# MLP in eighths with seven block products for eight, and an in-place start, in a two-layer trunk kernel

## The chip, the cores and the metric

The kernel runs on 1 core of one Trainium2 chip. The time is the device time of that core in microseconds (us); every kernel is compared with the kernel before on the same chip. PE is TensorE, DVE is VectorE, ACT is ScalarE, POOL is GpSimd, SP is SyncE.

## The reference

Two layers over x of 512 frames by 1024 channels (float32). Each layer adds a mix of four head groups, a cross-attention over 256 memory rows, and an MLP of width 4096; a last RMSNorm follows.

```
for l in range(DEPTH):                                # DEPTH = 2
    h = rmsnorm(x, norm_mix[l])
    z = h @ w_in[l]                                   # split into the four groups
    ...                                               # retention, RG-LRU, latent attention, gated delta rule
    x = x + jnp.concatenate([y_a, y_b, y_c, y_d], axis=-1) @ w_out[l]
    x = x + memory_xattn(rmsnorm(x, norm_xattn[l]), rmsnorm(mem, norm_mem[l]), xa_wq[l], xa_wkv[l], xa_wo[l])
    h = rmsnorm(x, norm_mlp[l])
    x = x + jnp.square(jax.nn.relu(h @ mlp_w1[l])) @ mlp_w2[l]
return rmsnorm(x, final_norm)
```

## The kernel before

x lies transposed: eight tiles `xr[0]` to `xr[7]` of 128 channels by 512 frames. Every large product is made of three matmuls, since each fp32 operand is split into a high and a low part: `mm3_cm` (L288) issues high x high, high x low and low x high into one PSUM bank. Weights come from DRAM in units of 128 x 1024 words (512 KB), in the order of a list, `PLAN`. `wload` (L263) issues for a unit an SP DMA into `wr`, an ACT copy that rounds it to the high part `wh`, and a DVE subtract that gives the low part `wl`; `wnext` (L280) keeps this two units ahead. `wr` and `wl` have two buffers, `wh` has three.

The helpers record every operation, so that all matmuls have line L235 (`mm`), all DVE and POOL tensor_tensor L220 (`tt`), all activations L232 (`act`), scalar_tensor_tensor L223 (`stt`). Tiles are told apart by names. PSUM banks carry the tags `pj` (2), `gd` (2), `ch` (3) and `lg` (1). A scheduler orders the instructions of each engine by priorities of lanes.

**The start.** `norm_tile` (L373) makes from each `xr[k]` the parts `xh` and `xl`, and `square_acc` squares it on ACT (`sq`) and adds it into `acc`, on POOL for the first seven. The projection `gdn` reads four weight units (`proj_g`, L304); `rstd_of` (L384) sums `acc` over the partitions by matmuls, takes the inverse root by a bit trick and three Newton steps on DVE, and `bcast` (L394) spreads it by matmuls and an ACT copy (`bc`). The first step of the delta rule, `xt`, needs `bc`. `rope_tables` (L425), some 25 DVE operations of 128 x 128, is issued before layer 0.

**The MLP.** After `xo` (the output projection of the cross-attention) `norm_tile` makes `xh`, `xl` and `acc` for it. It runs in two halves of 2048 hidden channels. For each of 16 tiles of 128 channels, w1 takes 8 x 3 matmuls of 128 x 512 and an evacuation (ACT Relu `r`, DVE `s`, ACT `hh`, DVE `hl`); then w2 takes for each of 8 output tiles 16 x 3 matmuls of 128 x 512, DVE multiplies the bank with `r2` (the inverse mean square, from `rstd`) into `t_`, and POOL (first half) or DVE adds `t_` to `xr[m]`.

**The end.** `last_tile` does the eighth output tile of the last layer in two halves of 256 frames, sums squares into `acch`, takes the root, broadcasts it, multiplies all eight `xr` halves (DVE and POOL) and writes 16 DMAs from the SP queue.

Of the kernel before, what the change touches and what calls it, by code (L numbers as in the profile page):

```python
# [20 lines left out]
S = 512  # L21
NL = 2
# [25 lines left out]

class Spec:
# [6 lines left out]
KORD = (1, 3, 2, 0)  # L56
DIAG = ((0, 0), (1, 1), (0, 1), (1, 0))


def plan():  # L60
# [106 lines left out]
def build(tc, A, out, dbg=None):  # L167
# [92 lines left out]
    wstate = dict(loaded=0, used=0, tiles={})  # L260
    total = NL * len(PLAN)

    def wload():  # L263
# [72 lines left out]

    def rsqrt(o, v, n):
# [46 lines left out]
    def rstd_of(acc, ntt=TT):  # L384
        ps = sct()
        for t in range(ntt):
            mm(ps[:, t:t + 1], acc[:, t * 128:(t + 1) * 128], ones, True, True)
# [37 lines left out]
    def rope_tables():  # L425
        with tc.tile_pool(name="rp", bufs=1) as rp:
            N = TT * 32
            pf = rp.tile([128, TT], F32, name="pf")
            V.tensor_copy(pf, posi)
            h = rp.tile([128, N], F32, name="rh")  # L430
            lo = rp.tile([128, N], F32, name="rl")
            n = rp.tile([128, N], F32, name="rn_")
            tt(V, h.rearrange("p (t f) -> p t f", t=TT), pf.unsqueeze(2).to_broadcast([128, TT, 32]),
               C("invf").unsqueeze(1).to_broadcast([128, TT, 32]), MU)
            V.memset(lo, 0.0)
            big = 12582912.0
# [30 lines left out]
    def layer(l):  # L467
# [41 lines left out]
        with lane(*GDN):  # L509
            rstd = rstd_of(acc)  # L510
            rstdh = o16("rstdh", 4)
            ts(V, rstdh, rstd, 0.5, MU)
        pg = proj_g("gdn", xh, xl, [pjt, pjt, cht, cht])
        with lane(*GDN):
            rbc = bcast(rstd)
# [706 lines left out]
        def residual_proj(name, srch, srcl, gname, units=(0, 1, 2, 3), pre=None, post=None, new=None):  # L1222
# [13 lines left out]
        def last_tile(facc, hh, hl, r2):  # L1236
            ws = [wnext(f"w217_{k0}") for k0 in (0, 8)]
            pss = [pst(), pst()]
            accs, rs = {}, {}

            def prod(g, ks):
                s = slice(g * 256, g * 256 + 256)
                for k in ks:
                    wh, wl = ws[k // 8]
                    c = slice(k % 8 * 128, k % 8 * 128 + 128)
                    mm3_cm(pss[g][:, 0:256], wh[:, c], wl[:, c], hh[k][:, s], hl[k][:, s], k == 0, k == 15)

            def evac(g):
                s = slice(g * 256, g * 256 + 256)
# [251 lines left out]
```

## Time and profile before

| | us |
|---|---|
| median of 3 runs | 1639.4 (1637.24 to 1642.54) |
| time of the profiled execution | 1640.58 |
| its span in the trace | 1638.4 |
| PE busy | 1595.0 (97%) |
| DVE busy | 905.5 (55%) |
| ACT busy | 679.8 (41%) |
| POOL busy | 116.4 (7%) |

The span is the time between the first and the last record; 2.2 us of the profiled execution lie outside it. Busy times are sums over instructions. A chain row gives a start, a length and the instructions that ran one behind the other.

### The profile page before, as it was taken

How to read it: one execution, taken by the hardware profiler on the slowest of the kernel's cores; microseconds unless marked ns; L12 is line 12 of the kernel's file. 1: busy time of each engine (PE TensorE's matmuls, PEld its weight loads, DVE VectorE, ACT ScalarE, POOL GpSimd, SP SyncE). 2: the span in 40 equal slices, each digit the busy share in tenths (PEclk: the TensorE clock that was granted, in tenths of full speed). 3: DMA queues.
4: the chain of work that ended last, by engine and by line, in shares of the span. 5: the costliest groups of instructions: out<-in, count | busy, mean ns of one | idle time of the engine just before them, and what ended most of it. 6: DMA issues, size and time to landing. Idle time of an engine off the chain costs nothing.

```text
span 1638.4 us, 22678 instructions
## 1 busy us (share of the span) xinstructions
PE 1595.0 (97%) x8920; PEld 1330.1 (81%) x8920; DVE 905.5 (55%) x1949; ACT 679.8 (41%) x1163; POOL 116.4 (7%) x112
## 2 busy tenths in 40 slices
PE   6999999999999999999999999999999999999997
PEld 5868889888888888888887788988888888888886
DVE  6788688456455422443367957754564543234333
ACT  5556544344343312432335646444454432134331
POOL 2001000110110010000101000002002000100011
PEclk8999999999999999999999989999999999999998
DMA  4202034332122222233332111254312232333322
GB/s 162 94 26 66 24 104 139 132 116 78 52 94 100 90 98 96 91 102 109 124 99 68 52 53 59 82 168 129 102 40 90 91 103 90 97 96 96 98 91 77
DMA packets 47914, 150.61 MB, mean 92 GB/s; under 512 B 5696, under 2 KB 9792, under 8 KB 47808
## 3 DMA queue, kind: packets, MB, share of 16 engines
q1 hardware_dynamic: 47808, 149.16, 28.2%
q8 instruction: 70, 1.15, 0.3%
q14 instruction: 36, 0.29, 0.1%
HBM read 144.95 MB, written 4.19 MB: 91 GB/s over the span
## 4 chain that ended last, share of the span: by engine, by line
PE 85%; DVE 8%; DMA 3%; ACT 2%; issue 1%; POOL 0%; SPq 0%; POOLq 0%; ACTq 0%; DVEq 0%
PE ch L235 28%; PE pj L235 24%; PE gd L235 23%; PE lg L235 8%; DMA wr<-in_wu 2%; DVE wl L220 1%; PE ch L403 1%; DMA mem<-in_memT 1%; ACT wh L232 1%; DVE g L648 1%; DVE g L684 0%; DVE xt L223 0%; DVE xt L220 0%; DVE bf L229 0%; DVE g L220 0%
## 5 line engine op out<-in xcount | busy, mean ns | idle before, releaser
L220 DVE TENSOR_TENSOR wl<-wr,wh 128x1024 fp32r<-128x1024 f32 (+1 forms) x256 | 311.4, 1216 | 555.4 <-PE pj L235 174.1
L232 ACT ACTIVATE wh<-wr 128x1024 fp32r<-128x1024 f32 (+1 forms) x256 | 269.6, 1053 | 616.8 <-PE pj L235 190.8
L235 PE MATMUL pj<-xh,wh 128*128 128x512 f32 x288 | 115.2, 400 | 7.1 <-ACT wh L232 7.1
L220 POOL TENSOR_TENSOR acc<-acc,sq 128x512 f32<-128x512 f32 x42 | 64.9, 1546 | 765.5 <-ACT sq L232 765.5
L235 PE MATMUL pj<-xh,wl 128*128 128x512 f32 x288 | 114.8, 399 | 0.0
L235 PE MATMUL pj<-xl,wh 128*128 128x512 f32 x288 | 114.3, 397 | 0.0
L235 PE MATMUL ch<-xh,wh 128*128 128x512 f32 x272 | 106.9, 393 | 0.0
L235 PE MATMUL ch<-xl,wh 128*128 128x512 f32 x272 | 106.6, 392 | 0.0
L235 PE MATMUL ch<-xh,wl 128*128 128x512 f32 x272 | 106.4, 391 | 0.0
L235 PE MATMUL pj<-wl,xh 128*128 128x256 f32 (+1 forms) x352 | 105.9, 301 | 0.0
L235 PE MATMUL pj<-wh,xl 128*128 128x256 f32 (+1 forms) x352 | 104.7, 298 | 0.0
L235 PE MATMUL pj<-wh,xh 128*128 128x256 f32 (+1 forms) x352 | 104.3, 296 | 0.0
L235 PE MATMUL ch<-hh,wh 128*128 128x512 f32 x192 | 75.8, 395 | 0.0
L235 PE MATMUL ch<-hl,wh 128*128 128x512 f32 x192 | 75.8, 395 | 0.0
L235 PE MATMUL ch<-hh,wl 128*128 128x512 f32 x192 | 75.8, 395 | 0.0
L235 PEld LDWEIGHTS pj<-xh,wh 128*128 128x128 f32 x288 | 55.0, 191 | 18.6 <-ACT wh L232 7.1
L235 PEld LDWEIGHTS pj<-wl,xh 128*128 128x128 f32 x352 | 68.0, 193 | 2.2 <-issue 1.0
L235 PEld LDWEIGHTS pj<-wh,xl 128*128 128x128 f32 x352 | 68.1, 193 | 1.4 <-issue 0.7
L235 PEld LDWEIGHTS pj<-wh,xh 128*128 128x128 f32 x352 | 68.2, 194 | 1.1 <-issue 0.2
L220 DVE TENSOR_TENSOR hl<-s,hh 128x512 fp32r<-128x512 f32 x64 | 44.3, 692 | 39.2 <-ACT hh L232 39.0
L235 PEld LDWEIGHTS pj<-xh,wl 128*128 128x128 f32 x288 | 54.9, 191 | 12.1 <-DVE wl L220 0.8
L235 PEld LDWEIGHTS pj<-xl,wh 128*128 128x128 f32 x288 | 54.9, 191 | 11.1 <-DVE xl L223 0.2
(545 smaller groups left out, 3754.1 us busy)
## 6 DMA issues: line engine op xcount, KB each, us to landing
wr<-in_wu SPq DMA_DIRECT2D x248, 512.0 KB, 3.4
x<-in_xT SPq DMA_DIRECT2D x16, 256.0 KB, 3.6
wr<-in_wu SPq DMA_DIRECT2D x8, 360.0 KB, 2.9
mem<-in_memT SPq DMA_DIRECT2D x16, 128.0 KB, 3.2
xs<-x SPq DMA_DIRECT2D x8, 256.0 KB, 2.7
x<-xs SPq DMA_DIRECT2D x8, 256.0 KB, 3.0
out<-x SPq DMA_DIRECT2D x16, 128.0 KB, 1.8
big<-in_wmla SPq DMA_DIRECT2D x2, 640.0 KB, 6.4
```

The costliest lines, as they stand in the source:

```text
L220: e.tensor_tensor(o, a, b, op=op)
L232: ACT.activation(o, i, f, **k)
L235: PE.matmul(o, lhsT=l, rhs=r, start=st, stop=sp, **k)
L403: PE.transpose(o, i, ident)
L648: V.transpose(Nt3[32 * q:32 * q + 32].rearrange("m j i -> m i j"), src)
```

## The change

Four parts.

1. **Start.** DVE zeroes `acc`, and three matmuls of zeros run on PE ahead of the first product. The first weight unit is cut in two halves (DMA, ACT and DVE each). The squares are taken in place in `xr` (it is loaded again later, as before), and added on DVE, no longer on POOL. They are issued ahead of gdn's third unit, `rstd_of` ahead of the fourth, `bcast` behind it. The rope tables are issued behind `rstdh`, in a buffer of the delta rule. In layer 1 the root comes ahead of the third unit.
2. **w1 by seven products.** The operand x is cut into 2 x 2 blocks (channels 0 to 511 and 512 to 1023; frames 0 to 255 and 256 to 511), w1 likewise for each 256 hidden channels. `prep` forms four differences of x blocks for each pair of tiles (POOL for the first three pairs, DVE for the last), `combo` splits seven block operands into high and low parts. `wload` forms four sums of weight blocks (`sm`) on POOL, splits 768 raw columns into `ah`, `al` and the 1024 columns of sums into `wh`, `wl`. `sprod` issues for each unit 2 x 7 x 3 = 42 matmuls of 128 x 256, where before a unit took 24 of 128 x 512. `spost` puts the four result blocks together from four banks: an ACT copy `p1` and five DVE additions into `W`; `sact` does Relu, square and the split in one instruction each over 1024 columns.
3. **Eighths.** The MLP goes by 512 hidden channels: w1 of the next eighth interleaves with w2 of this one by units. After each eighth DVE multiplies 8 banks by `r2` into `t_` (2 buffers), and POOL adds `t_` to `xr` (DVE in the last eighth). `rstd_of` and `bcast` of the MLP come in eighth 1.
4. **End.** The last four tiles are done by (half, tile) blocks of 12 matmuls of 128 x 256; squares go into the sum by matmuls, not by additions; the root is ACT Sqrt, a reciprocal and one Newton step (`rsqrt1`); output DMAs alternate between the ACT and SP queues.

```diff
+def sw_units(name, w, c0, lead):
+    def unit(i, g):
+        ks, a, b = (2 * g, 2 * g + 1), c0 + i * 256, c0 + i * 256 + 128
+        blocks = [(k, a) for k in ks] + [(k + 4, a) for k in ks] + [(k + 4, b) for k in ks] + [(k, b) for k in ks]
...
+            raw = sw.tile([128, n], F32, tag="sr", name=nm("sr"), bufs=2)
...
+            tt(G, s1, a21, a22, AD)
+            tt(G, s2, s1, a11, SU)
+            tt(G, s4, a12, s2, SU)
+            tt(G, s3, a11, a21, SU)
...
+            act(ah, raw[:, 0:768], AF.Copy)
+            tt(V, al, raw[:, 0:768], ah.bitcast(F32), SU)
...
+            act(hi, sm, AF.Copy)
+            tt(V, lo, sm, hi.bitcast(F32), SU)
...
+    def rsqrt1(o, v, n):
...
+        act(o, v, AF.Sqrt)
+        ts(V, nv, v, -0.5, MU)
+        V.reciprocal(o, o)
+        tt(V, w, o, o, MU)
+        tt(V, w, w, nv, MU)
+        stt(o, w, 1.5, o, AD, MU)
...
+    for n in (512, 512, 256):
+        mm(wps[:, 0:n], warm[:, 0:128], warm[:, 0:n], True, True)
...
+    def first_acc():
+        for k in range(KT):
+            act(xr[k] if k else xg[2], xr[k], AF.Square)
+            if k:
+                tt(V, xg[2], xg[2], xr[k], AD)
...
+        def norm_in(u):
+            if l == 0 and u == 2:
...
+                    first_acc()
+            if u == (3 if l == 0 else 2):
...
+                    rs_["r"] = rstd_of(acc)
...
+        def sprod(h, i, g, bk):
+            ah, al, sh, sl = wnext(f"w1{h}{i}_{g}")
+            for dj in range(2):
+                j = 2 * g + dj
+                for n_, b_, x_ in PRD:
...
+                    mm(o, wh[:, c], cmb[j][0][x_], first, False)
+                    mm(o, wh[:, c], cmb[j][1][x_], False, False)
+                    mm(o, wl[:, c], cmb[j][0][x_], False, last)
+
+        def spost(bk):
...
+            act(p1, blk(bk[3], 0), AF.Copy)
...
+            tt(V, W7[:, 0:5:4, :], two(bk[0]), bc2(p1), AD)
+            tt(V, W7[:, 5:7, :], two(bk[1]), bc2(blk(W, 4)), AD)
+            tt(V, blk(W, 3), blk(bk[1], 0), blk(W, 6), AD)
+            tt(V, blk(W, 2), blk(bk[2], 0), blk(W, 6), AD)
+            tt(V, blk(W, 1), blk(bk[2], 1), blk(W, 5), AD)
...
+        def sact(C, hh, hl):
+            hi, lo = hp4(), hp4()
+            act(C, C, AF.Relu)
+            act(C, C, AF.Square)
+            act(hi, C, AF.Copy)
+            tt(V, lo, C, hi.bitcast(F32), SU)
...
+        setA = lambda: [bank(t) for t in ("pj", "pj", "gd", "gd")]
+        setB = lambda: [bank(t) for t in ("ch", "ch", "ch", "lg")]
...
+        def evac(m, ps, fin):
+            t_ = mp.tile([128, S], F32, tag="t_", name=nm("t_"), bufs=2)
+            tt(V, t_, ps, st["r2"], MU)
+            tt(V if fin else G, xr[m], xr[m], t_, AD)
...
+        for e in range(9):
...
+                    w1_unit(e, i, g)
+                    if e == 1 and q == 0:
+                        st["rstd"] = rstd_of(acc, new=lambda: bank("gd"))
+                if e:
+                    w2_unit(e - 1, q)
```

Where this puts instructions, at three places. In the changed kernel `tt` has line L234, `act` L246, `stt` L237, `mm` L249.

DVE at the start, before: behind the last `xl` the first rope operations (`rh`, `rn__186`, `rl`) stand ahead of the last addition into `acc`, the others between the steps of the root (`rv`, `rt` and what follows).

```order
L220 TENSOR_TENSOR rh<-pf,cst 128x128
L227 TENSOR_SCALAR spn_1760<-sp_365_1759 128x2
L229 TENSOR_SCALAR rn__186<-rh 128x128
L227 TENSOR_SCALAR sp_365_1759<-sp_365_1759 128x2
L227 TENSOR_SCALAR rn__186<-rn__186 128x128
L220 TENSOR_TENSOR acc_137<-acc_137,sq_173 128x512
L223 SCALAR_TENSOR_TENSOR rh<-rn__186,rh 128x128
L223 SCALAR_TENSOR_TENSOR rl<-rn__186,rl 128x128
L223 SCALAR_TENSOR_TENSOR rh<-rn__186,rh 128x128
L229 TENSOR_SCALAR rv_227<-gd_222 128x4
L229 TENSOR_SCALAR rn__186<-rh 128x128
L227 TENSOR_SCALAR rt_230<-rv_227 128x4
```

The same place now, from the last Newton step of the root on (`rw`, `rstd`): the rope operations (`rope_299`) begin behind `rstdh`, ahead of the first `xt`; the others follow between the next `xt` and `g` operations.

```order
L234 TENSOR_TENSOR rw_283<-rstd_281 128x4
L234 TENSOR_TENSOR rw_283<-rw_283,rn_284 128x4
L237 SCALAR_TENSOR_TENSOR rstd_281<-rw_283,rstd_281 128x4
L579 TENSOR_SCALAR rstdh_297<-rstd_281 128x4
L492 CAST rope_299<-posi 128x4
L495 MEMSET rope_299 128x128
L234 TENSOR_TENSOR rope_299<-rope_299,cst 128x128
L243 TENSOR_SCALAR rope_299<-rope_299 128x128
L241 TENSOR_SCALAR rope_299<-rope_299 128x128
L237 SCALAR_TENSOR_TENSOR rope_299<-rope_299 128x128 x3
L234 TENSOR_TENSOR xt_370<-pj_171,bc_364 128x512
```

What moved: the rope operations went from in front of and within the root to behind it; the seven additions into `acc` stand ahead of it, all on DVE.

DVE in eighth 2 (counted from 0), where w1 of a block of 256 channels ends and w2 of eighth 1 runs (`al`, and `wl` from `sm`: splits of the weight units to come; `W`: the result blocks; `t_`: output tiles). Behind each row stand the engines and queues that it waits for.

```order
L234 TENSOR_TENSOR al_5857<-sr_5849,ah_5856 128x768 [waits DMAHW2_49,PE_49]
L234 TENSOR_TENSOR W_5789<-pj_5637,p_1139_5790 128x2x256 [waits PE_49,Activation_49]
L234 TENSOR_TENSOR wl_5744<-sm_5734,wh_5743 128x1024 [waits DVE_49,PE_49]
L234 TENSOR_TENSOR W_5789<-pj_5638,W_5789 128x512 [waits DVE_49]
L234 TENSOR_TENSOR t__1145_5833<-ch_5704,r_1076_5415 128x512 [waits PE_49,Pool_49]
L234 TENSOR_TENSOR W_5789<-pj_5638,W_5789 128x256 [waits DVE_49]
L234 TENSOR_TENSOR W_5789<-gd_5639,W_5789 128x256 x2
L234 TENSOR_TENSOR t__1146_5836<-ch_5705,r_1076_5415 128x512 [waits PE_49,Pool_49]
L234 TENSOR_TENSOR t__1147_5839<-ch_5706,r_1076_5415 128x512 [waits PE_49,Pool_49]
L234 TENSOR_TENSOR wl_5799<-wr_5797,wh_5798 128x1024 [waits DMAHW3_49,PE_49,Activation_49]
L234 TENSOR_TENSOR t__1148_5842<-lg_5707,r_1076_5415 128x512 [waits Pool_49]
```

Every one of these is new in its place: a weight split (`wl_5744`) stands between the parts of `W`, and each `t_` from the second row on waits for POOL to have freed one of two buffers.

ACT in eighth 1, around the copy `bc` of the broadcast bank (`p_`: the copy `p1`; `W`<-`W`: Relu, then square; `hp`: high part).

```order
L246 ACTIVATE p_1068_5365<-gd_5186 128x256 [waits PE_49]
L246 ACTIVATE ah_5531<-sr_5524 128x768 [waits DMAHW4_49,PE_49]
L246 ACTIVATE wh_5373<-wr_5372 128x1024 [waits DMAHW3_49,DVE_49,PE_49]
L246 ACTIVATE W_5364<-W_5364 128x1024 [waits DVE_49]
L246 ACTIVATE W_5364<-W_5364 128x1024 [waits Activation_49]
L246 ACTIVATE wh_5444<-sm_5435 128x1024 [waits PE_49,Pool_49]
L246 ACTIVATE hp_5402<-W_5364 128x1024 [waits Activation_49]
L246 ACTIVATE bc_5413<-gd_5408 128x512 [waits PE_49]
```

Before, the same copy stood in half a, with 512-column evacuations around it; now it stands behind four 1024-column operations, and the bank that it reads (`gd`, of which there are two) is the one that the third product of the next w1 block takes.

## Rows read from the trace of the kernel before

**Rows 1.** The page: busy engines, granted clock in 40 slices, and the chain.

```profile
PE 1595.0 (97%) x8920; PEld 1330.1 (81%) x8920; DVE 905.5 (55%) x1949; ACT 679.8 (41%) x1163; POOL 116.4 (7%) x112
...
PEclk8999999999999999999999989999999999999998
...
PE 85%; DVE 8%; DMA 3%; ACT 2%; issue 1%; POOL 0%; SPq 0%; POOLq 0%; ACTq 0%; DVEq 0%
```

**Rows 2.** The chain in the MLP of layer 0: start us, length us, instructions.

```profile
500.67 5.44 PE ch L235 x24
...
566.26 11.20 PE ch L235 x48
```

**Rows 3.** The chain in the last product and its evacuation.

```profile
1612.38 5.70 PE pj L235 x48
```

**Rows 4.** Windows, layer 0's MLP: length, busy us of each engine, clock, DMA.

```profile
466.00:821.00 355.00, 355.00 (x1553) 290.01 (x1552) 147.76 (x178) 114.39 (x146) 20.48 (x20) 1.00 0.30 100
```

**Rows 5.** Groups by shape: busy us, mean ns of one, idle before.

```profile
L220 DVE TENSOR_TENSOR wl<-wr,wh 128x1024 fp32r<-128x1024 f32 x248 | 304.1, 1226 | 549.1 <-PE pj L235 171.3 <-PE ch L235 133.9 <-issue 93.9
L220 DVE TENSOR_TENSOR wl<-wr,wh 128x720 fp32r<-128x720 f32 x8 | 7.3, 907 | 6.3 <-PE pj L235 2.7 <-PE ch L235 2.1 <-ACT g L232 1.4
...
L220 DVE TENSOR_TENSOR t__1120_5579<-gd,r 128x512 f32<-128x512 f32 x1 | 0.7, 684 | 0.0
...
L220 DVE TENSOR_TENSOR o<-ch,bf 128x256 f32<-128x256 f32 x22 | 8.7, 417 | 0.3
...
L232 ACT ACTIVATE wh<-wr 128x1024 fp32r<-128x1024 f32 x248 | 263.2, 1061 | 609.9 <-PE pj L235 187.8 <-PE ch L235 184.5 <-PE gd L235 100.3
...
L220 POOL TENSOR_TENSOR xt<-xt,cst 128x256 f32<-128x256 f32 x6 | 4.0, 668 | 160.6 <-PE ch L403 79.5 <-DVE o L220 77.3 <-ACT mem L232 3.6
...
L220 POOL TENSOR_TENSOR x<-x,t__1120_5579 128x512 f32<-128x512 f32 x1 | 1.3, 1292 | 103.2 <-DVE t__1120_5579 L220 103.2
```

**Rows 6.** Timeline of DVE and POOL: start us, length us, idle before it.

```profile
12.65 1.81 POOL L220 TENSOR_TENSOR acc<-acc,sq 128x512 f32<-128x512 f32 x1 [2.58 <-ACT sq L232]
13.22 2.45 DVE L223 SCALAR_TENSOR_TENSOR xl<-x,par,xh 128x512 fp32r<-128x512 f32 x2
...
443.07 0.69 DVE L220 TENSOR_TENSOR x<-x,gd 128x512 f32<-128x512 f32 x1 [0.67 <-PE gd L235]
443.14 1.30 POOL L220 TENSOR_TENSOR acc<-acc,sq 128x512 f32<-128x512 f32 x1 [98.45 <-ACT sq L232]
```

**Rows 7.** Timeline of the start: PE, DVE, ACT.

```profile
7.07 0.80 PE L235 MATMUL pj<-xh,wh 128*128 128x512 f32 x1 [7.07 <-ACT wh L232]
...
12.74 0.40 PE L235 MATMUL ch<-xh,wh 128*128 128x512 f32 x1
...
26.37 0.28 DVE L223 SCALAR_TENSOR_TENSOR rh<-rn__186,rh 128x128 f32<-128x128 f32 x1
...
26.51 1.86 PE L235 MATMUL gd<-cst,acc 128*128 128x1 f32 x8 [6.79 <-DVE acc L220]
...
35.33 0.15 DVE L223 SCALAR_TENSOR_TENSOR rstd<-rw,rstd 128x4 f32<-128x4 f32 x1
...
37.43 0.60 ACT L232 ACTIVATE bc<-gd 128x512 f32<-128x512 f32 x1 [1.21 <-PE gd L235]
...
40.03 0.69 DVE L220 TENSOR_TENSOR xt<-pj,bc 128x512 f32<-128x512 f32 x1
```

**Rows 8.** The chain behind the start.

```profile
44.01 5.44 PE pj L235 x24
```

**Rows 9.** Timeline of the end.

```profile
1625.94 9.97 SPq L1267 DMA_DIRECT2D out<-x  x16
1626.28 0.61 PE L235 MATMUL gd<-cst,acch 128*128 128x1 f32 x4 [1.59 <-DVE acch L220]
...
1629.64 1.19 PE L235 MATMUL gd<-cst,rstd 128*128 128x128 f32 x4 [2.75 <-DVE rstd L223]
...
1631.34 1.75 DVE L220 TENSOR_TENSOR x<-x,gd 128x256 f32<-128x256 f32 x5 [1.85 <-ACT bc L232]
```

More of the change, by code (lines that the diff above doesn't have):

```diff
@@ L1220, in layer, with residual_proj @@
             SP.dma_start(out=xr[m], in_=A["xT"][:, m, :] if l == 0 else xs[m])
[L1222 removed]
+        def residual_proj(name, srch, srcl, gname, units=(0, 1, 2, 3), pre=None, post=None, new=None, order=range(8)):
             nonlocal xg
@@ new lines, in two_km @@
+        def two_km(e, half, k0):
+            wh, wl = wnext(f"w2{e}{half}k{k0}")
+            hh, hl = H[e]
+            if not k0:
+                st["W2"] = setB()
+            for m in range(4):
+                for dk in range(2):
+                    c = slice(dk * 512 + m * 128, dk * 512 + m * 128 + 128)
+                    mm3_cm(st["W2"][m], wh[:, c], wl[:, c], hh[k0 + dk], hl[k0 + dk], k0 + dk == 0, k0 + dk == 3)
+            if st["pend"]:
+                st["pend"].pop(0)()
+            return k0 > 0
@@ new lines, in w2_unit @@
+        def w2_unit(e, j):
+            half = "ab"[j // 2]
+            if e < 7 or half == "a":
+                if two_km(e, half, j % 2 * 2):
+                    if st["r2"] is None:
+                        b = bcast(st["rstd"], new=lambda: bank("gd"))
+                        st["r2"] = mp.tile([128, S], F32, name=nm("r2"))
+                        tt(V, st["r2"], b, b, MU)
+                    for m in range(4):
+                        evac(4 * (j // 2) + m, st["W2"][m], e == 7)
+                return
+            hh, hl = H[e]
+            if last:
+                if j == 2:
+                    last_tiles(st["facc"], hh, hl, st["r2"])
+                return
+            wh, wl = wnext(f"w2{e}{'bc'[j - 2]}k0")
+            for mi in range(2):
+                ps = cyb()
+                for k in range(4):
+                    c = slice(k * 256 + mi * 128, k * 256 + mi * 128 + 128)
+                    mm3_cm(ps, wh[:, c], wl[:, c], hh[k], hl[k], k == 0, k == 3)
+                evac(2 * j + mi, ps, True)
@@ new lines, in layer @@
+        for e in range(9):
+            if e == 8:
+                st["nx"] = nx = None if last else new_xg()
+                st["facc"] = xp.tile([128, S], F32, tag="acc", name=nm("acc")) if last else None
+            for q in range(4):
+                if e < 8:
+                    i, g = (q % 2, q // 2) if e == 0 else (q // 2, q % 2)
+                    if e == 0 and q == 3:
+                        for m in (2, 6, 3, 7):
+                            xo_sq(m)
+                    w1_unit(e, i, g)
[3 more added lines that the diff above has]
+                    w2_unit(e - 1, q)
```

374 lines of the change are left out of this document (235 added, 139 removed).

## Prediction

> **What bounds the kernel now.** The page comes first: PE is busy for 1595.0 of 1638.4 us, the clock row reads 9 almost throughout, and 85% of the chain that ended last is PE, against 8% DVE and 3% DMA [rows 1]. So the time is a number of matmuls times their spacing, plus the few places where PE waits. The chain by pieces gives the spacing. In w1 24 matmuls of 128 x 512 take 5.44 us, 226.7 ns each; in w2 48 take 11.20, 233.3 ns each [rows 2]. The only w2 tile that is done 256 frames at a time takes 5.70 us for 48, 118.75 ns each [rows 3]: half the columns cost 51 to 52% of the time. In the window over layer 0's MLP PE is busy for all of 355 us at full clock, with DVE at 147.76, ACT at 114.39 and POOL at 20.48 [rows 4]. Fewer columns on PE thus shorten the MLP, as long as the other engines keep pace. Outside it PE stands still at the start (6.79 us before the sums [rows 7]) and at the end.
>
> **w1.** A layer has 32 units. Before, 32 x 24 = 768 matmuls x 226.7 ns = 174.1 us. Now 32 x 42 = 1344 x 118.75 ns = 159.6 us: 14.5 less per layer, **-29.0** for two. That is not the full eighth (21.8 per layer), since short matmuls cost more per column. w2 keeps its 768 matmuls of 128 x 512, but in runs of 24 instead of 48; I leave it at 233.3 ns. If it ran like w1 it would give 768 x 6.6 ns = 5.1 per layer, 10.2 in all; that end is kept for the range.
>
> **The other engines in an eighth.** PE needs 4 x 42 x 118.75 ns + 4 x 24 x 233.3 ns = 42.4 us. Prices of [rows 5]:
> - DVE: four `al` of 768 columns (907 ns for 720, so 0.97) 3.9; four `wl` of sums and four of w2 at 1.226, 9.8; two `W` sets of 2 x 0.684 + 3 x 0.417, 5.2; two low parts of 1024 columns 2.5; eight `t_` at 0.684, 5.5. Sum 26.8.
> - POOL: 16 sums of 256 columns at 0.668, 10.7, and eight additions to `xr` at 1.292, 10.3. Sum 21.0.
> - ACT: four `ah` 3.2, eight `wh` 8.5, six 1024-column steps of the activation 6.4, two `p1` (an estimate: 0.38 for 256 columns, a quarter of `wh` and a little) 0.8. Sum 19.7.
>
> None reaches 42.4 alone. But DVE and POOL are not independent. At the start POOL adds from 12.65 to 14.46, and two `xl` of DVE that begin at 13.22 take 2.45 us, where DVE needs 0.684 for an operation of this size [rows 5]; at 443.07 a DVE addition that reads PSUM takes its 0.69 although POOL works from 443.14, and POOL its 1.30 [rows 6]. So an operation with both inputs in SBUF and a POOL operation exclude each other, one with a PSUM input does not. The Trainium skill, SBUF — State Buffer, section "SBUF: two separate sides", states this as a rule: a DVE operation with two SBUF inputs and a GpSimd operation that reads SBUF lock each other out for a whole instruction. By that rule the trace is explained (2.45 us against about 1.4 for two), and it speaks against a change that gives POOL more to do beside DVE. In a layer's MLP POOL goes from 20.48 us [rows 4] to 8 x 21.0 = 168. Here 16.1 of DVE's 26.8 us have two SBUF inputs (`al`, `wl`, low parts); with POOL's 21.0 the pair needs 37.1 of 42.4 us. It fits, with 5 us to spare.
>
> Fitting on average is not enough, since banks turn over. Let a w1 block end at T. DVE does `W` 0.68, a `wl` 1.23, `W` 0.68, a `t_` 0.68, then three `W` of 0.42 (the order fence of DVE), behind `p1` of 0.38 on ACT: the `gd` banks are free at about T + 4.9. PE has 24 matmuls of w2 (5.6) and two products (0.7) first, so it wants them at T + 6.3. The margin is 1.4 us, and one POOL addition in front of that `wl` or one late `t_` (two buffers, freed by POOL) takes 1.3 of it. Over some 30 such blocks I take **+4** in all; bounds are 0 and +20 (two POOL operations, 1.96, ahead at each block: 0.6 x 30 = 18).
>
> **Into w1.** Behind the last `xo` tile DVE has an addition, four differences and eight low splits for the last two pairs of tiles, some 8.4 us at [rows 5]; the units that need only the first two pairs, put first, keep PE for 2 x 4.99 = 10.0. Cost 0, bound +4 for both layers if POOL is late with its differences.
>
> **Root in eighth 1.** The w1 bank `gd` of the third product is the one in which `rstd` was spread. ACT frees it with `bc`, which stands behind `W` Relu, square, a `wh` and `hp`, all behind DVE's last `W` (the order fence of ACT). DVE's last `W`, with the small root operations between, is done at about T + 5.8; four ACT steps of 1.06 and `bc` (0.60 [rows 7]) follow, partly overlapping DVE: T + 10.4, where PE would want the bank at T + 7.2. Some 3 to 4 us per layer, with the one to two more us by which the weight split on DVE may be late: **+8** for two layers, bounds +2 (if ACT takes `bc` early) and +12. Nothing of it is in the trace of before, where the MLP ran through.
>
> **Start.** Before, the first product begins at 7.07, its first 12 matmuls last until 12.74, 0.47 us each, twice w1's 0.227, which is the lower of the clock's two levels (1.2 GHz) behind a PE that had done nothing; PE stands from 19.72 to 26.51 for DVE's last `acc`, the root ends at 35.33, `bc` begins at 37.43 and `xt` at 40.03 [rows 7], and PE leaves `gdn` at 44.01 [rows 8]. Now half a unit comes first, so the product can begin at about 6.1, behind the zeros, which I take to bring the full rate. Unit 1 waits for its split, which stands on ACT behind four conversions and two squares: 14.1. It ends at 19, unit 2 at 24.1; the squares and the seven DVE additions (0.68 each, as `t_`) are through at 24.4, the root, no longer interleaved with rope operations, at 28.9, unit 3 at 31.5. For PE that is 12.3 earlier. The delta rule's chain starts with `xt` at 30.8 instead of 40.03, 9.2 earlier, but some 25 rope operations (0.28, [rows 7], 7 us at most) are now between its first steps. What is passed on lies between: **-10.5**, bounds -6 (all rope operations on the chain, zeros of no use) and -13.
>
> **End.** From the sums to the last output: sums at 1626.28, then 2.75 us in which PE waits for the root, broadcast at 1629.64, products at 1631.34, end at 1638.4; the 16 output DMAs take SP's queue 9.97 us, 0.62 each [rows 9]. One Newton step instead of three and no bit trick makes 12 small operations 6, some 1.0; the last addition goes, 0.4; four of the last eight DMAs on a second queue are 1 to 2. **-3**, bounds -1 and -4.
>
> **Sum.** 1640.6 (the profiled execution; 1.2 above the median) - 29.0 + 4 + 8 - 10.5 - 3 = 1610.1. Taken against the median it would be 1609; I say **1610**.
>
> **Rivals.**
> - *No stalls* (chance 0.13): POOL fits into the gaps, `bc` is in time, and w2 in short runs goes like w1. 1640.6 - 29 - 13 - 4 + 2 = 1597, less up to 10: 1587 to 1600. For it: every average fits.
> - *The bank margin is too short* (0.22): `t_` with two buffers and POOL's additions hold `W` up in every block; +20 instead of +4 and +12 instead of +8: 1630, range 1617 to 1636. For it: 1.4 us of margin against 1.3 us operations. Against: most DVE work at that place reads PSUM.
> - *The start is not passed on* (0.08): the mix stage is paced by DVE, not by PE, and takes the rope operations in full: 1615 to 1621.
> - *DVE becomes the bound through POOL* (0.06): if DVE stood still for every POOL operation, an eighth would need 26.8 + 21.0 = 47.8 us, 5.4 over PE's, 86 over 16 eighths: 1692. It decides for slower from about 31 us over both layers, 1.9 per eighth, that is if POOL stops DVE for more than 17.5 of its 21.0 us per eighth. Range 1637 to 1692. The rule of the Trainium skill quoted above gives this case if it held for all of DVE's operations. Against: of DVE's work 10.7 us reads PSUM and isn't stopped.
>
> The forecast has 0.51 (its own range 1601 to 1617). The range for 8 in 10 goes from 1592, inside the first rival, to 1633, inside the second. Within 0.3% (5 us, about what a measurement can tell from no change) lies the edge between the second and the last rival: 0.03. Slower: 0.05. Faster: 0.92.
>
> **What would show it.** In the changed profile: w1 units of 42 matmuls in 4.99 us on the chain; PE busy near 97%; POOL's busy time up to some 440 us; DVE waits of `wl` and `al` behind POOL; one gap on PE of 3 to 4 us per layer released by ACT `bc`; the first `xt` near 31. Wrong it would be if the 256-column matmuls, four banks in turn, are further apart than 118.75 ns (3 ns are 8 us in all), if PE shows a gap at each block released by DVE `W`, or if the delta rule leaves its stage no earlier than before.

## The result and the profile after

The changed kernel takes 1620.6 us (median of 4 runs, 1619.25 to 1624.71) against 1640.0; the ratio is 0.9894, 95% interval 0.9875 to 0.9912. 1610 was forecast in a range of 1592 to 1633: the direction and the main term were right, and two thirds of the gain came. The page of the profile, as in [rows 1]:

```profile
PE 1574.2 (97%) x10094; PEld 1366.5 (84%) x10094; DVE 1134.7 (70%) x2197; ACT 784.2 (48%) x1269; POOL 502.2 (31%) x473
...
PE 74%; DVE 13%; issue 4%; ACT 3%; POOL 3%; DMA 3%; SPq 0%; POOLq 0%; DVEq 0%; ACTq 0%
```

PE lost only 21 us of busy time; POOL has four times its work, DVE a quarter more, and DVE, ACT and POOL have more of the chain (13, 3 and 3%; before 8, 2 and 0). Where the time came from is read by stages. In this table, worked out from the traces, a stage runs from the first matmul of one product to the first of the next: to `wout` of layer 0; `wout` and attention; `xo`; the MLP (its last matmul ends it); layer 1's mix stage, and in brackets the delta rule's solve inside it; and from the last product to the end of the span.

```
kernel                   mix 0  attn 0  xo 0  MLP 0   mix 1 (solve)  attn 1  xo 1  MLP 1   end     span
before                   287.2  135.2   43.5  355.2   267.6 (26.9)   135.9   43.5  355.9   14.2   1638.4
changed                  274.9  136.6   43.7  348.1   268.8 (25.5)   136.5   43.7  352.9   13.4   1618.5
e1 sums on DVE           275.2  135.3   43.7  347.1   265.9 (22.4)   135.2   43.7  351.9   12.8   1610.8
e2 differences on DVE    276.4  136.5   43.6  346.0   270.3 (26.8)   136.5   43.6  349.5   13.1   1615.6
e3 both on DVE           274.0  135.3   43.6  345.3   271.1 (28.4)   135.3   43.7  348.6   13.1   1609.8
e4 start alone           275.9  135.3   43.6  355.2   263.3 (22.4)   136.2   43.5  355.9   14.0   1622.9
e5 no zeros              278.0  136.6   43.7  348.4   268.1 (26.8)   136.5   43.7  354.8   13.3   1623.1
e6 sums twice            276.3  136.5   43.7  369.8   265.1 (22.4)   136.5   43.7  375.1   12.6   1659.3
e7 root a tile later     274.8  136.5   43.7  348.3   265.4 (22.5)   136.5   43.7  350.5   13.5   1613.0
e8 e3 and e7             275.7  135.2   43.7  344.4   270.0 (26.9)   135.3   43.7  345.7   12.9   1606.5
e9 e8, squares on DVE    275.5  135.2   43.6  340.5   263.6 (22.5)   135.2   43.6  342.3   13.9   1593.5
e10 long roots           273.5  136.5   43.7  348.2   271.2 (28.4)   136.5   43.7  353.3   15.2   1621.7
e11 e8, three buffers    273.4  135.2   43.6  343.1   265.3 (23.9)   135.2   43.7  345.4   13.2   1598.2
e12 e9 and e11           273.0  135.2   43.6  340.4   262.4 (22.5)   135.2   43.7  342.2   13.8   1589.6
```

The start gave 12.3, the MLPs 7.0 and 3.1, the end 0.8; attention took back 1.3 and 0.6, layer 1's mix stage 1.1. The solve's brackets move with the granted clock (last section) and belong to no kernel. Other stages also differ between profiles of the same instructions: mix 0 took 273.0 to 276.4 us in the twelve profiles with this start, so its 12.3 could be read as 10.8 to 14.3, and MLP 1 took 352.9 in the changed kernel and 354.8 in e5, which differs from it only at the start. Layer 0's MLP and attention repeat within 0.3 us.

**The steady MLP is as forecast.** Windows of the changed kernel: an eighth; all of layer 0's MLP, beside [rows 4]; and four stretches of the turn from `xo` to w1.

```profile
600.00:642.40 42.40, 42.40 (x266) 38.19 (x265) 29.54 (x32) 18.56 (x20) 25.61 (x25) 1.00 0.31 101
...
455.18:803.32 348.14, 343.14 (x2130) 308.05 (x2128) 247.67 (x288) 155.96 (x176) 200.06 (x183) 1.00 0.29 96
...
461.00:466.20 5.20, 5.17 (x43) 5.17 (x44) 2.68 (x3) 4.28 (x7) 5.08 (x6) 1.00 0.00 0
466.20:469.60 3.40, 0.31 (x3) 0.10 (x1) 3.40 (x7) 1.58 (x2) 0.69 (x1) 0.98 0.00 0
469.60:476.00 6.40, 6.37 (x41) 6.37 (x42) 4.95 (x5) 0.85 (x1) 2.71 (x4) 0.74 0.50 166
476.00:486.10 10.10, 10.10 (x85) 9.97 (x85) 8.04 (x14) 8.15 (x10) 8.99 (x9) 1.00 0.35 110
```

The columns are length, then busy us of PE, PE's weight loads, DVE, ACT and POOL, granted clock, DMA share and GB/s. An eighth of 42.4 us has PE busy for all of it: 118.75 and 233.3 ns per matmul hold. DVE and POOL stretch to 29.5 and 25.6 (26.8 and 21.0 were worked out): they stop each other, and it is hidden. The MLP of layer 0 is 1344 x 118.75 + 768 x 233.3 ns = 338.8 us of products and, as before, some 1.8 of root and broadcast; 7.5 us are lost, most of it in the turn (0.9 more is a wait of the first w2 product for its low part, at 486.5). There PE stands from 466.2 to 469.6, and then the mean clock is 0.74: 13 products are 0.213 us apart, the lower level (1.2 GHz), behind a PE that had stood 3.1 us.

**The turn.** Timeline of the changed kernel, from where DVE begins the splits for the third of the four pairs of tiles:

```profile
453.67 5.02 DVE L234 TENSOR_TENSOR cxl<-hp,cxh 128x512 fp32r<-128x512 f32 x4 [0.52 <-ACT cxh L246]
458.62 1.76 DVE L234 TENSOR_TENSOR wl<-sm,wh 128x1024 fp32r<-128x1024 f32 x1
460.30 0.67 DVE L234 TENSOR_TENSOR x<-x,lg 128x512 f32<-128x512 f32 x1
...
454.93 2.07 POOL L234 TENSOR_TENSOR hp<-hp,hp 128x256 f32<-128x256 f32 x2
456.96 2.33 POOL L234 TENSOR_TENSOR sm<-sr 128x256 f32<-128x256 f32 x2
459.26 1.71 POOL L234 TENSOR_TENSOR sm<-sm,sr 128x256 f32<-128x256 f32 x1
461.04 0.73 POOL L234 TENSOR_TENSOR sm<-sr,sm 128x256 f32<-128x256 f32 x1
...
461.81 1.06 ACT L246 ACTIVATE wh<-sm 128x1024 fp32r<-128x1024 f32 x1 [3.62 <-POOL sm L234]
462.78 0.71 ACT L246 ACTIVATE hp<-x,par 128x512 f32<-128x512 f32 x1
...
468.63 0.94 DVE L234 TENSOR_TENSOR al<-sr,ah 128x768 fp32r<-128x768 f32 x1
...
461.03 0.38 PE L249 MATMUL lg<-cxh,ah 128*128 128x256 f32 x1 [0.70 <-DVE x L234]
...
469.63 0.58 PE L249 MATMUL gd<-cxh,al 128*128 128x256 f32 x1 [3.12 <-DVE al L234]
```

Read it as two queues that hold each other up. Four splits, three of 0.69 and one of 0.42 us alone, take 5.02 us beside POOL's differences and sums, a `wl` 1.76 instead of 1.23, and POOL's third sum 1.71 instead of 0.67. So the last `xo` tile, done on PE by 455.2, is added to x on DVE only at 460.30. ACT meanwhile waits 3.62 us for POOL's last sum, with the scaling of that tile (`hp`, 462.78) queued behind the wait. The differences, splits and `al` of DVE come last, and PE waits for `al`.

**Attention.** The sums of the first two w1 units are prefetched into it:

```profile
394.72 1.44 POOL L234 TENSOR_TENSOR sm<-sr 128x256 f32<-128x256 f32 x2 [62.32 <-PE pj L249]
...
395.44 0.86 DVE L241 TENSOR_SCALAR Pm<-Pm,sm 128x256 f32<-128x256 f32 x1
396.23 0.69 DVE L234 TENSOR_TENSOR nb<-mx,nrs 128x1 f32<-128x1 f32 x1
```

In the kernel before the same two softmax steps took 0.35 and 0.15 us on average:

```profile
L227 DVE TENSOR_SCALAR Pm<-Pm,sm 128x256 f32<-128x256 f32 x32 | 11.0, 348 | 0.4
...
L220 DVE TENSOR_TENSOR nb<-mx,nrs 128x1 f32<-128x1 f32 x32 | 4.4, 150 | 0.1
```

The stage, which is a chain on DVE, gets 1.3 us longer in layer 0.

**The root in eighth 1** cost next to nothing: `bc` was late by 0.26 us, not 3 to 4.

```profile
508.10 0.38 PE L249 MATMUL gd<-cxh,ah 128*128 128x256 f32 x1 [0.26 <-ACT bc L246]
...
507.47 0.57 ACT L246 ACTIVATE bc<-gd 128x512 f32<-128x512 f32 x1
```

**The start**, beside [rows 7]: `xt` begins at 31.09, and PE begins the next unit at 32.50 instead of 44.01 [rows 8].

```profile
6.10 0.73 PE L249 MATMUL pj<-xh,wh 128*128 128x512 f32 x2 [0.34 <-ACT wh L246]
...
9.93 0.73 PE L249 MATMUL pj<-xh,wh 128*128 128x512 f32 x2 [2.17 <-ACT xh L246]
...
10.50 0.39 PE L249 MATMUL ch<-xh,wh 128*128 128x512 f32 x1
10.73 0.40 PE L249 MATMUL ch<-xl,wh 128*128 128x512 f32 x1
...
31.09 0.69 DVE L234 TENSOR_TENSOR xt<-pj,bc 128x512 f32<-128x512 f32 x1 [0.48 <-ACT bc L246]
```

**The end**, beside [rows 9]:

```profile
1597.09 0.35 PE L249 MATMUL gd<-cst,acc 128*128 128x1 f32 x2 [1.05 <-DVE acc L234]
...
1609.34 0.15 DVE L234 TENSOR_TENSOR rw<-rw,rn 128x2 f32<-128x2 f32 x1
1609.41 0.41 DVE L234 TENSOR_TENSOR x<-x,gd 128x256 f32<-128x256 f32 x1
1609.74 0.15 DVE L237 SCALAR_TENSOR_TENSOR rstd<-rw,rstd 128x2 f32<-128x2 f32 x1
1610.03 1.19 PE L249 MATMUL gd<-cst,rstd 128*128 128x128 f32 x4 [2.42 <-DVE rstd L237]
```

From 1595.75 to 1599.2 PE does one product; otherwise it waits for the sums of the first half's root and does their 12 one-column matmuls; 16 products behind it are 0.213 us apart. In the second half each small step of the root stands behind a 0.41 us product, so PE waits 2.42 us for a root of half the steps, 2.75 before.

### The profile page after: what moved, and what is told of

It is laid out like the page before. It is cut to its first block, busy times and chain, and to the rows that moved or that the text cites. A ratio compares the mean times of both kernels' runs of the same rounds, so it can differ in the third digit from the quotient of the medians.

```text
span 1618.5 us, 25948 instructions
## 1 busy us (share of the span) xinstructions
PE 1574.2 (97%) x10094; PEld 1366.5 (84%) x10094; DVE 1134.7 (70%) x2197; ACT 784.2 (48%) x1269; POOL 502.2 (31%) x473
## 3 DMA queue, kind: packets, MB, share of 16 engines
q10 hardware_dynamic: 1152, 1.05, 0.2%
## 4 chain that ended last, share of the span: by engine, by line
PE 74%; DVE 13%; issue 4%; ACT 3%; POOL 3%; DMA 3%; SPq 0%; POOLq 0%; DVEq 0%; ACTq 0%
PE ch L249 25%; PE pj L249 23%; PE gd L249 18%; PE lg L249 7%; DVE wl L234 2%; DMA wr<-in_wu 2%; POOL hp L234 1%; PE ch L454 1%; ACT wh L246 1%; POOL sm L234 1%; POOL acc L234 1%; DVE x L234 1%; DMA mem<-in_memT 1%; DVE Pm L241 0%; ACT hp L246 0%
## 5 line engine op out<-in xcount | busy, mean ns | idle before, releaser
L234 DVE TENSOR_TENSOR wl<-wr,wh 128x1024 fp32r<-128x1024 f32 (+2 forms) x193 | 257.5, 1334 | 228.8 <-issue 74.1
L246 ACT ACTIVATE wh<-wr 128x1024 fp32r<-128x1024 f32 (+2 forms) x193 | 201.4, 1044 | 252.9 <-DMA wr<-in_wu 74.8
L249 PE MATMUL ch<-hp,wh 128*128 128x512 f32 (+1 forms) x768 | 238.4, 392 | 0.9 <-DVE hp L234 0.9
L234 POOL TENSOR_TENSOR sm<-sr 128x256 f32<-128x256 f32 x128 | 99.7, 800 | 343.4 <-PE pj L249 133.4
L249 PEld LDWEIGHTS ch<-hp,wh 128*128 128x128 f32 x768 | 140.4, 189 | 29.3 <-DVE hp L234 1.5
L249 PE MATMUL ch<-hp,wl 128*128 128x512 f32 (+1 forms) x384 | 150.4, 392 | 0.0
L234 POOL TENSOR_TENSOR acc<-acc,sq 128x512 f32<-128x512 f32 x33 | 52.9, 1603 | 299.5 <-ACT sq L246 299.5
L246 ACT ACTIVATE wh<-sm 128x1024 fp32r<-128x1024 f32 x64 | 67.4, 1053 | 124.9 <-PE lg L249 110.7
L234 DVE TENSOR_TENSOR al<-sr,ah 128x768 fp32r<-128x768 f32 x64 | 89.4, 1397 | 50.4 <-PE gd L249 50.3
L246 ACT ACTIVATE W<-W 128x1024 f32<-128x1024 f32 x64 | 67.7, 1059 | 80.0 <-DVE W L234 79.1
L249 PE MATMUL pj<-wl,xh 128*128 128x256 f32 (+1 forms) x352 | 106.5, 303 | 0.0
L249 PE MATMUL pj<-wh,xl 128*128 128x256 f32 (+1 forms) x352 | 104.5, 297 | 0.0
L249 PE MATMUL pj<-wh,xh 128*128 128x256 f32 (+1 forms) x352 | 103.0, 293 | 1.4 <-DVE gd L237 1.3
L249 PE MATMUL pj<-cxh,wl 128*128 128x256 f32 x360 | 102.5, 285 | 0.4 <-DVE wl L234 0.4
L249 PE MATMUL pj<-cxh,wh 128*128 128x256 f32 x360 | 102.1, 284 | 0.0
L249 PE MATMUL pj<-cxl,wh 128*128 128x256 f32 x360 | 101.4, 282 | 0.0
L249 PEld LDWEIGHTS ch<-hp,wl 128*128 128x128 f32 x384 | 72.4, 189 | 16.1
L234 DVE TENSOR_TENSOR wl<-sm,wh 128x1024 fp32r<-128x1024 f32 x64 | 80.3, 1254 | 4.0 <-PE gd L249 2.9
L249 PE MATMUL lg<-hp,wh 128*128 128x512 f32 (+1 forms) x256 | 78.9, 390 | 0.0
L246 ACT ACTIVATE ah<-sr 128x768 fp32r<-128x768 f32 x64 | 53.9, 846 | 49.3 <-PE gd L249 37.2
L249 PE MATMUL gd<-cxh,al 128*128 128x256 f32 x240 | 68.4, 285 | 6.2 <-DVE al L234 6.2
L249 PEld LDWEIGHTS pj<-wh,xh 128*128 128x128 f32 x352 | 67.6, 192 | 2.9 <-DVE gd L237 1.8
```

What stands on the lines that cost most here:

```text
L234: e.tensor_tensor(o, a, b, op=op)
L246: ACT.activation(o, i, f, **k)
L249: PE.matmul(o, lhsT=l, rhs=r, start=st, stop=sp, **k)
```

## The experiments

Theory L: the missing 10 us are where POOL operations and DVE operations with two SBUF inputs shut each other out at places that nothing covers. Theory W: DVE and ACT simply have too much to do there. Ratios are to the kernel before on the same chip (its medians were 1638.7 to 1640.7 us), with 95% intervals. Only one execution of each kernel has a trace, so a difference by stages is one of that execution, not of the median.

**e1, the weight sums on DVE.**

```diff
-            tt(G, s1, a21, a22, AD)
+            tt(V, s1, a21, a22, AD)
```

(and so for `s2`, `s4`, `s3`).

> The four weight sums of each w1 unit go from POOL to DVE; the rest is the changed kernel (1620.6). Theory L (the changed kernel loses time where POOL operations shut DVE out: 1.3 us in each attention, 6 to 7 us in each turn from xo to w1): the attention loses its 1.3 us, the turn gets shorter by 1 to 3 us per layer, the steady eighths stay at 42.4 us (DVE has 33.5 of 42.4): 1612 to 1617. Theory W (the turn is long because DVE and ACT have too much to do there, whoever POOL is): eight more operations of 0.42 us stand on DVE in each turn, 3.4 us per layer: 1624 to 1629.

1609.4 us, ratio 0.9825 (0.9804 to 0.9846), below L's range. Attention is back at 135.3 and 135.2 us. In the changed kernel no engine waits there for a result of POOL's, so that loss was the exclusion itself. MLP 0 is 1.0 shorter, MLP 1 0.9, the low edge of L, and the eight more DVE operations per turn cost nothing net. But in the turn the wait moved. PE's wait before `al`, 3.1 us, is 0.1, and in layer 0 it now waits longer for `x` (0.70 before) and for `W` (none before):

```profile
461.52 0.39 PE L249 MATMUL lg<-cxh,ah 128*128 128x256 f32 x1 [2.16 <-DVE x L234]
...
479.94 0.39 PE L249 MATMUL gd<-cxh,ah 128*128 128x256 f32 x1 [1.99 <-DVE W L234]
```

So e1 bears out L in attention; in the turn it only shows that W's 3.4 us per layer did not come. Of the 7.7 us between the two traces 3.0 are the solve's.

**e2, the differences on DVE.**

```diff
-            E = V if j == 3 else G
+            E = V
```

> The differences of x blocks for the first three pairs of tiles go from POOL to DVE, as for the fourth; weight sums stay on POOL. Theory L: POOL's sums come some 5 us earlier in the turn, ACT's copy of them no longer holds up the last scaling of x, the idle 3.1 us of PE before al goes to below 1: 3 to 5 us less per layer, 1611 to 1615. Theory W: 4.6 us more on DVE per turn, PE idles longer: 1624 to 1630. The attention keeps its 1.3 us either way.

1616.9 us, 0.9864 (0.9844 to 0.9884), above L's range and far below W's. MLP 0 falls by 2.2, MLP 1 by 3.3, where L said 3 to 5. PE's wait of 3.1 us before `al` is 0.8 in both layers, as forecast, but waits of 0.9 and 0.8 us for W's banks stand in the trace; e5 and e7, whose MLPs up to the last tiles are the changed kernel's, have such waits too, so they are not clearly e2's doing. L's direction, at less than its size.

**e3, both.**

> Both moves: POOL is left with the squares of xo and the additions to x. Theory L: both gains, the PE gap at the turn below 1 us and the attention as before the change: 1606 to 1613. Theory W: 8 us more work on DVE per turn: 1630 or more.

1610.3 us, 0.9828 (0.9802 to 0.9854). W's 1630 is excluded. By stages it is better than e1 (MLPs 5.1 us less); in the traced executions its solve was 6.0 longer, so that the two spans are only 1.0 apart. What is left in the turn is a wait of PE of 2.1 us for `W`, in layer 0.

**e4, the start alone**, on the kernel before (the diff's parts on the first unit, zeros, squares, root and rope tables).

> The kernel before (1640.0) with the new start alone: halved first unit, zeros, squares in place on DVE, late broadcast, rope tables behind the root, and layer 1's root ahead of the third unit. If the start is passed on to the end in full, as the two traces' first product of wout says (287.23 before, 274.92 after: 12.3 earlier), 1627 to 1630. If the mix stage takes part of it back, 1631 to 1635. Layer 1's mix stage took 1.1 us longer in the changed kernel; if the earlier root there is the reason, it shows here too.

1624.6 us, 0.9911 (0.9892 to 0.9930), 14.4 less. Mix 0 gives 11.3; layer 1's mix is 4.3 shorter, of which the solve is 4.5. So the start is passed on in full, and the earlier root in layer 1 costs nothing there: the changed kernel's longer mix 1 is not its doing. By the medians the start alone has 14.4 of the changed kernel's 19.4 us. The other three parts, forecast at -20 together, are left with some 5, and the intervals of the two ratios overlap.

**e5, without the zeros.**

```diff
-    V.memset(warm, 0.0)
...
-    for n in (512, 512, 256):
-        mm(wps[:, 0:n], warm[:, 0:128], warm[:, 0:n], True, True)
```

> The changed kernel (1620.6) without the zeroing of acc and the three matmuls of zeros; the rest of the start is as changed. If the zeros bring the full rate to the first products, these run at half rate again: PE waits anyway until 9.93 for the second block of x, then some 12 to 25 products of unit 0 take 0.21 us more each, 2.5 to 5 us, and since PE went from unit 2 into the sums without a wait, most of it is passed on: 1622 to 1625. If the wait until 9.93 already undoes what the zeros did, or the sums have slack, within 1 us of the changed kernel.

1624.6 us, 0.9912 (0.9888 to 0.9935), as forecast, though this interval overlaps the changed kernel's. The trace is clearer: mix 0 is 278.0, 3.1 longer than in the changed kernel and 1.6 longer than in any of the twelve profiles with the zeros, and `xt` begins at 33.64, in those at 29.46 to 31.10. Its timeline of PE:

```profile
9.91 0.80 PE L249 MATMUL pj<-xh,wh 128*128 128x512 f32 x1 [2.14 <-ACT xh L246]
...
11.71 0.63 PE L249 MATMUL pj<-xh,wh 128*128 128x512 f32 x1
12.14 0.63 PE L249 MATMUL pj<-xl,wh 128*128 128x512 f32 x1
```

Products behind the same wait of 2.1 us start 0.43 us apart here and 0.23 in the changed kernel (10.50 and 10.73 above): zeros ahead of the wait buy the upper clock level (2.4 GHz) behind it. The level is read from the spacing, since the window views give a granted clock of 1.00 there in both kernels.

**e6, the sums twice** in eighths 2 to 7.

```diff
+            for _ in range(2 if int(PLAN[i][0][2]) > 1 else 1):
                 tt(G, s1, a21, a22, AD)
```

(with the other three inside the loop).

> In the w1 units of eighths 2 to 7 POOL makes the four weight sums twice (same values written again); nothing else. POOL goes to 31.7 us per eighth, beside PE's 42.4. Theory L with durations as they stand: DVE's operations with two SBUF inputs and POOL need 16.1 + 31.7 = 47.8 us, PE waits some 5 us in each of these eighths, 40 to 65 us in all: 1660 to 1685. Theory A (an average below PE's is hidden, exclusion or not): 1620 to 1625.

1662.2 us, 1.0141 (1.0114 to 1.0168): slower than the kernel before. PE's waits over the whole span, a window of 42.4 us, one of a whole eighth, and a wait of DVE:

```profile
PE ch L249 <- DVE wl L234: 19.0, 20, 1.0
PE pj L249 <- DVE wl L234: 14.9, 25, 1.7
...
600.00:642.40 42.40, 39.36 (x238) 34.30 (x237) 28.12 (x32) 14.79 (x17) 37.76 (x35) 1.00 0.25 87
587.90:634.30 46.40, 43.36 (x264) 38.04 (x264) 28.44 (x33) 18.56 (x20) 41.76 (x40) 1.00 0.27 91
...
601.95 0.69 DVE L234 TENSOR_TENSOR t__1215_6283<-ch,r 128x512 f32<-128x512 f32 x1 [5.63 <-POOL x L234]
```

DVE got no new work and is at 28 of 42.4, POOL at 38; neither is full, yet PE waits 34 us in all for DVE's `wl`. The eighth takes 46.4 us, and each MLP grows by 22 us, 3.6 per eighth on average. Theory A falls: an average below PE's is not hidden. The sum of what excludes itself, DVE's 16.1 and POOL's 31.7 us, is 47.8 and over PE's 42.4, where the changed kernel stood at 37.1. This is the last rival of the prediction, made real, with only part of DVE's work stopped. That the sum alone sets the 46.4 is not shown: DVE also stands 5.63 us at a `t_` until POOL's addition to x, queued behind the doubled sums, frees one of two buffers, and no run separates POOL's order from the sum.

**e7, the sums of the first half's root a tile later.**

```diff
-            rs[0] = rstd_of(p0, 2, rsqrt1)
             tile(1, 5)
+            rs[0] = rstd_of(p0, 2, rsqrt1)
```

> The changed kernel with the sums of the first half's root issued one tile of the second half later, at the end of the last layer. In the changed kernel's trace PE stands 1.1 us there for an addition on DVE, and the 16 matmuls behind run at half rate (0.213 us for 0.119). If the wait is the cause, the wait goes, and the time falls by 1 to 3 us: 1617.5 to 1619.5. If the one-column matmuls of the sums themselves are (12 of them, 2 us), nothing changes.

1614.7 us, 0.9855 (0.9830 to 0.9879), below the range expected. MLP 1 is 2.3 shorter, the wait of 1.05 us is gone (one of 0.47 for ACT's squares comes instead) and all but one of the products behind the sums are back at the upper level; 3.0 of the rest is the solve. The wait and the lower clock behind it were about half of the 4 us lost there.

**e8, e3 and e7 together.**

> Sums and differences on DVE and the root a tile later. If the gains add, 1 to 3 us under the run with both on DVE (1610.3): 1607 to 1609.

1608.2 us, 0.9804 (0.9774 to 0.9835). The gains add: MLP 1 345.7, solve 26.9.

**e9, the squares on DVE too.**

```diff
-        tt(G if k < KT - 1 else V, acc, acc, sq, AD)
+        tt(V, acc, acc, sq, AD)
```

> The kernel of the run with all on DVE and the root later (1608.2), with every addition of squares on DVE too, so that POOL is left with the additions to x in the MLP and the last products. Theory L: DVE's splits in the turn and in the last eighth are no longer stopped by 1.3 to 1.9 us additions: 1 to 4 us less, 1604 to 1607. Theory W: 14 more DVE operations of 0.68 in turn and end: 1609 to 1614.

1597.6 us, 0.9755 (0.9723 to 0.9786), below L's range. Of the 13.0 us between the traces of e8 and e9 the MLPs have 3.9 and 3.4, the solve 4.4, the rest of mix 1 2.0. Windows over both MLPs:

```profile
454.42:794.88 340.46, 340.46 (x2129) 306.54 (x2128) 284.48 (x407) 154.97 (x175) 82.15 (x62) 1.00 0.28 99
1237.32:1579.58 342.26, 342.26 (x2191) 310.43 (x2189) 284.66 (x417) 158.16 (x183) 80.00 (x56) 1.00 0.26 90
```

PE has no idle time in either: the 340.5 us are the 338.8 of products and 1.8 of root. DVE is busy 284 us, where it was 248 in the changed kernel. More DVE work and no wait: W is out. Only once, for 0.8 us, does ACT wait for a square of POOL's in the turn of e8, so here, as in attention, POOL beside DVE was most of the cost. For sums and differences the runs do not separate that from POOL being late with what ACT waits for (3.62 us in the changed kernel's turn): moving them takes both away.

Mix 1 without its solve is 241.1 us, 243.3 in the changed kernel. Its first root begins 16.6 us into the stage and its solve at 116.0 to 116.2 in all ten profiles with POOL's squares ahead of it; here, and in e12, they begin at 12.8 and 114.7. So 1.4 us go with the squares. The remainder lies behind the solve, where profiles differ from 125.3 to 127.4 us whatever POOL does (e5, with the changed kernel's instructions, has 125.3).

**e10, long last roots.**

```diff
-            rs[0] = rstd_of(p0, 2, rsqrt1)
+            rs[0] = rstd_of(p0, 2)
```

(and so for `rs[1]`).

> The changed kernel (1620.6) with the bit trick and three Newton steps in both last roots instead of Sqrt, reciprocal and one step. The prediction took 1.0 us for the short root. In the changed trace PE waits 2.42 us for the last root against 2.75 before, since each of its small operations on DVE stands behind a 0.41 us product of the first half: if these products set the pace, the long root costs 0.5 us or less more; if the number of operations does, 1 to 1.5 us more: 1621 to 1622.5.

1621.5 us, 0.9897 (0.9869 to 0.9924), no different by the median; by the trace the end is 15.2 instead of 13.4 (12.6 to 13.4 in the six profiles whose end is the changed kernel's), and PE's last wait for `rstd` 3.9 instead of 2.4. The number of steps does count: the short root is worth 1.5 us by the wait, 1.8 or more by the stage.

**e11, three raw buffers**, on e8.

```diff
-            raw = sw.tile([128, n], F32, tag="sr", name=nm("sr"), bufs=2)
+            raw = sw.tile([128, n], F32, tag="sr", name=nm("sr"), bufs=3)
```

> The kernel with all on DVE and the root later (1608.2) with three instead of two buffers for the raw w1 units. In its trace the fourth unit lands only after the second is given back, and its split falls together with the first W on DVE, for whose banks PE waits 1.7 us in layer 0. If the late landing is the cause, 0.5 to 2 us less per layer: 1604 to 1607. If DVE is simply full in the turn, no change.

1599.9 us, 0.9768 (0.9741 to 0.9794). In layer 0's turn PE's wait for `W` falls from 1.6 to 0.3 us, so the late landing was a cause; e9 loses the same wait without a third buffer. By the traces 8.3 us came: 1.3 in MLP 0, as expected, only 0.3 in MLP 1, and 3.0 in the solve, 2.3 in mix 0 and 1.7 in the rest of mix 1, which the edit does not touch.

**e12, e9 and e11 together.**

> The last two together: sums, differences and squares on DVE, the root a tile later, three raw buffers. With the squares on DVE alone layer 0's MLP takes 340.47 us where its matmuls need 338.8 and the root 1.8, so nothing is left there for a third buffer; layer 1's has 1.8 us more, some of it at the end. 1595 to 1599, not distinguishable from the run with squares on DVE (1597.6).

1594.4 us, 0.9755 (0.9730 to 0.9780), by the medians 44 us under the kernel before and 26 under the changed kernel, not told apart from e9.

## Why the prediction was right in direction and short in size

The number lies in the stated range, but above the forecast's own 1601 to 1617 and inside the ranges of two rivals, banks (1617 to 1636) and a start not passed on (1615 to 1621), neither of which happened. That it is not further off is partly luck: 12 us for banks and root, of which under 1 came, stood in for some 15 in the turns and 6 at the end that the sum did not have.

- **w1, -29.0, w2 unchanged.** Right to the row: 42.4 us per eighth, PE full. The products alone fall by 14.5 us per layer; in e9, where PE never waits, MLP 0 is 14.7 under the kernel before. (The prediction's sum for ACT, 19.7, adds up to 18.9; nothing rests on it.)
- **Banks, +4.** In the changed kernel's profile it was 0: the operations between the two `W` were stretched, but not beyond the margin of 1.4 us. The mechanism is real all the same, in the turn: e5 and e7 leave the MLP of layer 1 and of layer 0 as it is in the changed kernel, and PE waits there 1.25 and 0.89 us for a `W`. The waits of e6 are for `wl`, not for a bank.

```profile
1282.90 0.39 PE L249 MATMUL gd<-cxh,ah 128*128 128x256 f32 x1 [1.25 <-DVE W L234]
```

- **Into w1, 0.** This is the step that failed, in words "cost 0 ... the units that need only the first two pairs, put first, keep PE". It took most of 7.5 us per layer, where its bound was 4 for both. The 8.4 us of DVE work were priced as if alone; with the weight splits and waits between them they take from 453.67 to 470.18, twice that, while POOL makes differences, sums and squares, and ACT's wait for a sum was not seen at all. The prediction had stated the exclusion and applied it only to the average of an eighth. e9 shows the loss vanish with POOL's work moved away, at more DVE work.
- **Root in eighth 1, +8.** It was 0.5 in all. The wait is the one forecast, the term was too large: PE's wish for the bank was put at T + 7.2, and it came at T + 8.8 (508.1 less the wait of 0.26, in a block that ended at 499.1), since the broadcast's own matmuls and more products run ahead of it; ACT had `bc` done at T + 9.0.
- **Start, -10.5.** 12.3 to `wout`, inside the bounds; PE left `gdn` 11.5 us earlier, not 12.3, and `xt` came 8.9 earlier, not 9.2. The delta rule's solve began only 6.1 earlier (129.46 for 135.53), so between `xt` and the solve some of the lead is spent, whether on rope operations was not taken apart; by `wout` it is back. e4 bears out that the start is passed on, e5 what the zeros do.
- **End, -3.** From the last product on it was -0.8, and the wait for the first half's root with the slow products behind it took about 4 before that: +3 net. The root's shortening was sized at 1.0 and is worth at least 1.5 (e10), so other parts of the new end cost about 1 more than the old; which of them (12 one-column matmuls for 4, products between the root's steps) was not taken apart.
- **Not in the sum:** 1.3 and 0.6 us in attention, from POOL beside a chain of DVE (e1), and about 2.5 in layer 1's mix stage without its solve, of which 1.4 go with the squares on POOL (e9) and the rest differs between profiles.

The Trainium skill, SBUF — State Buffer, section "SBUF: two separate sides", states the exclusion for single instructions, and so it has to be asked at each place where a DVE chain is on the path, not of the mean. The trace agrees, with 0.69 for 0.15 us on a 128x1 operation. The Trainium skill, Perfetto Trace Analysis, section "Optimizing Scalar/DVE Operations", warns that moving work between DVE and GpSimd may not help; here moving it back to DVE, with the later root, gave 23 us by the medians (1620.6 to 1597.6) and 25.0 by the traces, 18.3 of them in the MLPs and 3.0 in the solve.

## What to carry to other kernels

Add up what excludes itself: DVE operations with two SBUF inputs and POOL's operations share one budget. Beside 42 us of PE a sum of 37 cost nothing in the steady eighths here, and one of 48 cost 3.6 per eighth; where between them the loss begins no run shows. Where DVE's chain is the path itself (a softmax, a turn between stages, a root), POOL beside it costs at once, and there an operation is better on DVE for 0.42 us than on POOL for 0.67. Price a turn between two stages as its own stage, with each queue's order written down. And before a difference of stages is given a cause, see how far that stage moves between profiles of the same instructions.

## What the runs showed of the hardware

The solve of the delta rule in layer 1 issues the same instructions in the same order on PE, DVE, ACT and POOL in all fourteen profiles, and takes 22.4 to 28.4 us. The windows around it, of e1 and of e3:

```profile
915.40:940.84 25.44, 23.67 (x380) 22.28 (x378) 19.42 (x35) 14.14 (x25) 2.25 (x4) 1.00 0.25 84
```

```profile
912.12:943.49 31.37, 29.60 (x380) 27.96 (x379) 19.43 (x35) 14.14 (x25) 2.24 (x4) 0.78 0.19 68
```

DVE and ACT have the same busy time, PE 5.9 us more, and the granted clock is 1.00 against 0.78: for part of the stretch PE runs at the lower of its two levels (1.2 GHz). Over the fourteen profiles the length follows the granted clock within the solve: 22.4 to 22.5 us at 1.00, 23.9 at 0.93, 25.5 at 0.87, 26.8 to 26.9 at 0.81 and 28.4 at 0.76, with PE idle for 1.7 to 1.8 us in each. What PE did ahead of it is the same in e1 and e3: it stands 1.0 us for ACT ahead of the solve and 1.7 for DVE inside it, and then does 62 small matmuls of 64 x 64. The products behind these are 0.12 us apart in e1 and 0.21 in e3. In layer 0 the same solve took 24.4 to 24.7 us at granted clocks of 0.93 to 1.00, with less idle time on PE at the lower one (0.2 us instead of 1.3). So a difference of 3 us between two medians, or 6 between two profiles, can be this alone; stages tell kernels apart where the whole does not, as long as their own spread is known.
